# The last six modulation tiles are made in the norm chain before the second feed-forward half, from weights loaded in the mixer's output stage

## Chip, cores and metric

One core of a Trainium2 chip runs the whole layer. The metric is the time of one execution on the device in microseconds (us). Matrix products run on TensorE (PE in the rows), elementwise work on VectorE (DVE), ScalarE (ACT) and GpSimd (POOL); SyncE (SP) issues nearly all transfers, in the order of its queue.

## What is computed

One layer of a hybrid backbone: 512 latent tokens (x) and 256 context tokens, 1024 channels. A modulation vector of 9 × 1024 numbers is made from the conditioning c, and the layer is a half-step feed-forward block, a mixer, and a second half-step feed-forward block:

```python
mx = [m[:, None, :] for m in adaln(c, w_ada[i], b_ada[i])]   # silu(c) @ w_ada + b_ada, split in 9
x = x + 0.5 * mx[2] * swiglu(modulate(rmsnorm(x, norm1_w[i]), mx[0], mx[1]), ffn1_w_in[i], ffn1_w_out[i])
ux = modulate(rmsnorm(x, norm2_w[i]), mx[3], mx[4])
...
mix_x = merge_branches(px, pool_grid(px[..., GATE_END:POOL_END]), ox, ...)
x = x + mx[5] * mix_x
x = x + 0.5 * mx[8] * swiglu(modulate(rmsnorm(x, norm3_w[i]), mx[6], mx[7]), ffn2_w_in[i], ffn2_w_out[i])
...
return rmsnorm(x, final_norm_w)
```

The mixer's merge is `(g_pool * y_pool + g_gdn * y_gdn) @ w_mix_out`, where the g are sigmoids of a projection (the branch gates), y_pool is a projection by w_pool_proj and y_gdn one by w_gdn_proj. What matters here: the ninth modulation part, mx[8], is needed only when the second feed-forward block adds to x.

## The kernel before

**The modulation.** w_ada is cut into 72 tiles of 1024 × 128, 512 KB each; tile t gives 128 of the 9216 modulation numbers, so tiles 64 to 71 give mx[8]. `ada_steps` makes two tiles, a pair: it loads both (SP, line 146), multiplies them with the conditioning vector `sc` (line 150: 16 small matmuls, which the trace counts as 32, since each runs in two passes), copies the product (VectorE, line 153, buffer `ada`), and after its `yield` transposes it (line 157), reduces and adds the bias (lines 159 and 162). Eight pairs are made at the start. The other 28 pairs wait in the list `ada_left`. `trickle` is called in the first feed-forward half at fixed places and makes the next pair there, whose second part follows at the next call; `LATE` = 2 pairs are kept for the end of that half. `mod_gate(1, 2, True)` and `mod_gate(1, 8, True)` scale the gate parts of the two feed-forward halves into `eff`.

**The first feed-forward half** computes with matmuls at line 345 in groups of output channels; each precise product is three matmuls of a high and a low part (names ending in hi and lo). VectorE and ScalarE split weights and activations, GpSimd helps.

**The mixer's output stage.** The last 11 of the 16 branch gates are made in the last steps of the scan loop: matmuls of line 132 (operands hhi, hlo), ScalarE's copy to `bgate` (line 1032), SP's write to `bg_dram` (line 1033). Then the stage begins: four tiles of y are read back (yg, line 1078), split into yphi and yplo (lines 188 and 189) and multiplied with w_pool_proj, whose tiles are loaded at line 110 and split at lines 119 and 120; the gates come back as gp and gg (lines 1083 and 1095) and get their sigmoid. Further yg, from yg_dram (line 1089), feed w_gdn_proj, and at the end w_mix_out updates the stream xl, which was loaded whole (line 1091, 2 MB).

**The norm chain.** Squares of xl are gathered in acc (line 197); TensorE sums them over channels (line 205, on bank b), VectorE and GpSimd make the reciprocal root (lines 177 and 179), VectorE spreads it on a diagonal (`diag`, line 209), TensorE broadcasts it (line 215), and VectorE and ScalarE make nt, xhi and xlo from it, with which the second half begins (line 279). `f0` are its first weights, loaded ahead.

**What sets the order.** The code is traced once; a scheduler lays out each engine's queue from the order in the code and from when buffers come free, and each engine then runs its queue in that order. All loads and writes of these stages go through SP's one queue.

## Time and profile before

| | us |
|---|---|
| median of 3 runs | 1752.39 |
| lowest and highest run | 1749.08 to 1753.36 |
| the profiled execution's own time | 1756.71 |
| its span | 1755.0 |
| TensorE busy | 1653.5 (94%) |
| VectorE busy | 1119.0 (64%) |
| ScalarE busy | 842.6 (48%) |
| GpSimd busy | 390.8 (22%) |

The span is the stretch between the first and the last recorded instruction of the profiled execution; a little time lies around it. TensorE is busy nearly throughout, so the few places at which it stands are those to look at. PEclk in the rows is the granted clock of TensorE as a share of the full 2.4 GHz: 1.00 is the upper level, 0.50 the lower, 1.2 GHz; values between are stretches with both.

### The profile page before, as it was taken

To read this page: it belongs to the slowest core of one execution; us is meant where nothing else is said; L and a number is where in the kernel's file an instruction comes from. 1 tells how busy PE (TensorE), PEld (TensorE's weight loads), DVE (VectorE), ACT (ScalarE), POOL (GpSimd) and SP (SyncE) were. 2 spreads that over 40 slices of the span, in tenths; PEclk is the share of its full clock that TensorE was granted. 3 is DMA by queue.
4 is the path that set the end of the run, shared out by engine and by line. 5 is a ranking of instruction groups with operands and counts; after the bars stand their busy time and mean duration, and the time that the engine had idled before them with its cause. 6 is when DMAs were issued, how large, how long until landed. Compare 5 with 4: busy or idle time off the path is not lost.

```text
span 1755.0 us, 31315 instructions
## 1 busy us (share of the span) xinstructions
PE 1653.5 (94%) x12220; PEld 1423.9 (81%) x12220; DVE 1119.0 (64%) x2254; ACT 842.6 (48%) x1851; POOL 390.8 (22%) x493
## 2 busy tenths in 40 slices
PE   6899999999999999889999999999998999999996
PEld 4889898989999778777878788787786788888885
DVE  5778888798888886375678767774555533333333
ACT  5443343434444364667677767665443322222233
POOL 2243444444454121123323331100000000000000
PEclk9999999999999999989999999999999999999998
DMA  9355536361221325532112212224654232333321
GB/s 273 112 155 151 156 96 182 103 189 65 78 67 56 108 82 187 138 100 67 44 52 65 60 45 53 56 61 154 214 158 116 69 98 88 94 96 96 93 64 48
DMA packets 282696, 183.82 MB, mean 105 GB/s; under 512 B 7008, under 2 KB 269877, under 8 KB 282421
## 3 DMA queue, kind: packets, MB, share of 16 engines
q1 hardware_dynamic: 282112, 181.65, 35.6%
q8 instruction: 96, 1.57, 0.4%
q14 instruction: 51, 0.42, 0.1%
q10 hardware_dynamic: 437, 0.18, 0.1%
HBM read 170.22 MB, written 11.58 MB: 104 GB/s over the span
## 4 chain that ended last, share of the span: by engine, by line
PE 71%; DVE 14%; ACT 5%; DMA 5%; POOL 2%; issue 2%; SPq 0%; ACTq 0%; POOLq 0%; DVEq 0%
PE b L132 22%; PE b L345 9%; PE a L132 6%; PE g L132 6%; PE a L345 5%; PE g L345 5%; DVE cv L583 2%; PE b L279 2%; PE a L279 1%; PE g L279 1%; PE a L708 1%; ACT din L848 1%; DVE wlo L120 1%; DMA bg_dram<-bgate 1%; PE b L150 1%
## 5 line engine op out<-in xcount | busy, mean ns | idle before, releaser
L188 ACT CAST fhi<-fst 128x512 fp32r<-128x512 f32 (+1 forms) x136 | 77.7, 605 | 249.6 <-PE b L132 85.6
L132 PE MATMUL b<-hhi,whi 128*128 128x512 f32 (+1 forms) x528 | 187.6, 384 | 0.0
L132 PE MATMUL b<-hlo,whi 128*128 128x512 f32 (+1 forms) x528 | 187.5, 383 | 0.0
L132 PE MATMUL b<-hhi,wlo 128*128 128x512 f32 (+1 forms) x528 | 186.9, 384 | 0.0
L179 POOL TENSOR_TENSOR rs<-rs,mhalf 128x4 f32<-128x4 f32 (+2 forms) x13 | 13.6, 1045 | 665.3 <-DVE rs L177 649.7
L189 DVE TENSOR_TENSOR flo<-fst,fhi 128x512 fp32r<-128x512 f32 (+1 forms) x136 | 87.3, 671 | 92.6 <-ACT fhi L188 92.4
L119 ACT CAST whi<-stg 128x512 fp32r<-128x512 f32 x146 | 89.4, 620 | 91.6 <-PE b L132 59.9
L119 ACT CAST whi<-qst 128x512 fp32r<-128x512 f32 (+1 forms) x160 | 81.6, 512 | 106.5 <-PE b L345 43.2
L119 ACT CAST whi<-qs 128x512 fp32r<-128x512 f32 (+1 forms) x120 | 59.5, 512 | 115.2 <-POOL qs L309 76.2
L583 DVE SCALAR_TENSOR_TENSOR cv<-raw,vec,cv 128x772 f32<-128x772 f32 (+1 forms) x96 | 101.6, 1058 | 11.6 <-ACT cv L581 8.3
L120 DVE TENSOR_TENSOR wlo<-qst,whi 128x512 fp32r<-128x512 f32 (+1 forms) x160 | 100.7, 639 | 10.1 <-ACT whi L119 10.0
L132 PEld LDWEIGHTS b<-hlo,whi 128*128 128x128 f32 x528 | 94.0, 190 | 14.8
L132 PEld LDWEIGHTS b<-hhi,whi 128*128 128x128 f32 x528 | 94.0, 190 | 14.8
L132 PEld LDWEIGHTS b<-hhi,wlo 128*128 128x128 f32 x528 | 93.3, 190 | 14.8
L308 POOL TENSOR_TENSOR qs<-qst 128x512 f32<-128x512 f32 (+1 forms) x40 | 46.4, 1161 | 247.2 <-DMA qst<-in_ffn_w_in_dram 76.6
L120 POOL TENSOR_TENSOR wlo<-stg,whi 128x512 fp32r<-128x512 f32 x46 | 65.4, 1430 | 90.6 <-ACT whi L119 70.6
L120 DVE TENSOR_TENSOR wlo<-stg,whi 128x512 fp32r<-128x512 f32 x100 | 68.2, 686 | 22.1 <-ACT whi L119 20.2
L188 ACT CAST ahi<-q 128x384 fp32r<-128x384 f32 x74 | 37.5, 512 | 75.4 <-DVE q L257 35.6
L120 DVE TENSOR_TENSOR wlo<-qs,whi 128x512 fp32r<-128x512 f32 (+1 forms) x80 | 49.0, 613 | 32.6 <-ACT whi L119 32.6
L132 PE MATMUL b<-xlo,fhi 128*128 128x512 f32 x160 | 63.4, 396 | 0.0
L132 PE MATMUL b<-xhi,flo 128*128 128x512 f32 x160 | 63.4, 396 | 0.0
L132 PE MATMUL b<-xhi,fhi 128*128 128x512 f32 x160 | 63.4, 396 | 0.0
(512 smaller groups left out, 4909.8 us busy)
## 6 DMA issues: line engine op xcount, KB each, us to landing
stg<-in_w_ada_dram SPq DMA_DIRECT2D x56, 512.0 KB, 4.0
stg<-in_w_mix_in_dram SPq DMA_DIRECT2D x49, 512.0 KB, 3.7
fst<-in_ffn_w_in_dram SPq DMA_DIRECT2D x44, 512.0 KB, 3.6
qst<-in_ffn_w_in_dram SPq DMA_DIRECT2D x40, 512.0 KB, 3.4
qst<-in_ffn_w_out_dram SPq DMA_DIRECT2D x40, 256.0 KB, 2.6
adx<-in_w_ada_dram SPq DMA_DIRECT2D x16, 512.0 KB, 6.4
fst<-in_ffn_w_out_dram SPq DMA_DIRECT2D x16, 512.0 KB, 3.9
crow<-cumd SPq DMA_DIRECT2D x16, 384.0 KB, 7.8
```

What stands on the lines that cost most here:

```text
L119: (first.copy if first is act else first.tensor_copy)(out=hi[:, :n], in_=w)
L120: second.tensor_tensor(out=lo[:, :n], in0=w, in1=hi[:, :n], op=ALU.subtract)
L132: pe.matmul(res[p][:, :m], lhsT=ww(i), rhs=hh(k)[:, o:o + m], start=(i == 0 and j == 0), stop=(i == n - 1 and j == 2))
L150: pe.matmul(b[32 * j:32 * j + 32, e * 128:(e + 1) * 128], lhsT=sc[:, k, :], rhs=stg[:, k, :], start=(i == 0), stop=(i == 1))
L188: act.copy(out=hi, in_=src)
L189: dve.tensor_tensor(out=lo, in0=src, in1=hi, op=ALU.subtract)
L279: pe.matmul(x, lhsT=ww(k), rhs=rhs(j, part, k), start=n + e == 0, stop=n + e == len(ks) + 1)
L308: pool.tensor_tensor(out=s1, in0=a21, in1=a22, op=ALU.add)
L345: pe.matmul(o, lhsT=ww[:, k], rhs=rhs(j, part, k), start=first and k + i == 0, stop=k + i == nh + 1, skip_group_check=not first)
L583: dve.scalar_tensor_tensor(out=cv[:, :n], in0=raw[:, t:t + n], scalar=tap[t], in1=cv[:, :n], op0=ALU.mult, op1=ALU.add)
L708: pe.matmul(r[:, :256], lhsT=hh[:, k, t * 128:(t + 1) * 128], rhs=ww[:, k], start=n == 0, stop=n == 3 * KT - 1)
L848: act.copy(out=din[o:o + 32, :, 0:12].rearrange("p f u -> p u f"), in_=L[o:o + 32, :, o:o + 32])
```

## The change

Tiles 66 to 71 leave `ada_left`, which now has 25 pairs, so three trickled pairs fewer are made in the first half (the number 24 in `trickle` becomes 21, so that the first gate is scaled after the same pair). Their six loads of 512 KB each are issued in the mixer's output stage into buffers of their own (pool `al`). In the norm chain the matmuls of the three pairs are put in fixed places: the first pair ahead of the sums, the second between the sums and the broadcast, the third behind the broadcast. Their transposes, reductions and additions follow after the first two hidden tiles of the second half are activated, and `mod_gate(1, 8, True)` after them. The copies of the products and `diag` are put into the loaded tiles, where these are done with; `sc` moves to a pool that lives to the end.

```diff
--- before.py
+++ after.py
@@ -82,7 +82,7 @@
     pool.memset(ones, 1.0)
     mhalf = base.tile([128, 32], F32, name="mhalf")
     pool.memset(mhalf, -0.5)
-    sc = xs.tile([128, KT, 32], F32, name="sc")
+    sc = base.tile([128, KT, 32], F32, name="sc")
     pool.memset(sc, 0.0)
     vb = bank("a")
     pe.transpose(vb[:, 0:16], cvec, ident[0:16, 0:16])
@@ -138,24 +138,29 @@
         for _ in ada_steps(cts, tags, room):
             pass
 
-    def ada_steps(cts, tags="bb", room=None):
+    def ada_steps(cts, tags="bb", room=None, loaded=None):
         b = bank(tags[0])
         for e, t in enumerate(cts):
-            pl_, tag, bufs = room or (wp, "stg", 2)
-            stg = pl_.tile([128, KT, 128], F32, tag=tag, name=tag, bufs=bufs)
-            sp.dma_start(out=stg, in_=a["w_ada"][:, t * 128:(t + 1) * 128].rearrange("(k p) m -> p k m", p=128))
+            if loaded:
+                stg = loaded[e]
+            else:
+                pl_, tag, bufs = room or (wp, "stg", 2)
+                stg = pl_.tile([128, KT, 128], F32, tag=tag, name=tag, bufs=bufs)
+                sp.dma_start(out=stg, in_=a["w_ada"][:, t * 128:(t + 1) * 128].rearrange("(k p) m -> p k m", p=128))
             for i in range(2):
                 for j in range(4):
                     k = 2 * j + i
-                    pe.matmul(b[32 * j:32 * j + 32, e * 128:(e + 1) * 128], lhsT=sc[:, k, :], rhs=stg[:, k, :],
-                              start=(i == 0), stop=(i == 1))
-        s = xs.tile([128, 256], F32, tag="ada", name="ada", bufs=1)
+                    ins = pe.matmul(b[32 * j:32 * j + 32, e * 128:(e + 1) * 128], lhsT=sc[:, k, :], rhs=stg[:, k, :],
+                                    start=(i == 0), stop=(i == 1))
+                    if loaded and i + j == 0:
+                        tc.keep_in_program_order(ins)
+        s = loaded[0][:, 0:2].rearrange("p k m -> p (k m)") if loaded else xs.tile([128, 256], F32, tag="ada", name="ada", bufs=1)
         dve.tensor_copy(out=s, in_=b[:, :256])
         yield
         b2 = bank(tags[1])
         for i in range(2):
             pe.transpose(b2[:, i * 128:(i + 1) * 128], s[:, i * 128:(i + 1) * 128], ident)
-        r = xs.tile([128, 2, 2], F32, tag="adar", name="adar", bufs=2)
+        r = (room if loaded else xs).tile([128, 2, 2], F32, tag="adar", name="adar", bufs=2)
         dve.tensor_reduce(out=r, in_=b2[:, :256].rearrange("p (t j s) -> p t s j", t=2, j=4)[:, :, :2, :],
                           axis=AX.X, op=ALU.add)
         for i, t in enumerate(cts):
@@ -196,15 +201,20 @@
             act.activation(out=sq, in_=src, func=AF.Square)
             dve.tensor_tensor(out=acc[:, :n], in0=acc[:, :n], in1=sq, op=ALU.add)
 
-    def rstd_rows(tmp, acc, parts, ssq=None, tag="b", dtag=("diag", 1)):
+    def rstd_rows(tmp, acc, parts, ssq=None, tag="b", dtag=("diag", 1), meanwhile=None, diag=None):
 
         n = sum(PARTS[p][1] for p in parts)
         if ssq is None:
             ssq = bank(tag)
             for i in range(n // 128):
-                pe.matmul(ssq[:, i:i + 1], lhsT=acc[:, i * 128:(i + 1) * 128], rhs=ones[:, 0:1])
+                ins = pe.matmul(ssq[:, i:i + 1], lhsT=acc[:, i * 128:(i + 1) * 128], rhs=ones[:, 0:1])
+                if meanwhile and not i:
+                    tc.keep_in_program_order(ins)
+        if meanwhile:
+            meanwhile()
         r = rstd_of(ssq[:, :n // 128], n // 128, D)
-        diag = tmp.tile([128, n], F32, tag=dtag[0], name="diag", bufs=dtag[1])
+        if diag is None:
+            diag = tmp.tile([128, n], F32, tag=dtag[0], name="diag", bufs=dtag[1])
         for i in range(n // 128):
             dve.tensor_scalar(out=diag[:, i * 128:(i + 1) * 128], in0=ident, scalar1=r[:, i:i + 1],
                               scalar2=None, op0=ALU.mult)
@@ -212,7 +222,9 @@
         for p in parts:
             m = PARTS[p][1]
             bs[p] = bank(tag)
-            pe.matmul(bs[p][:, :m], lhsT=ones, rhs=diag[:, o:o + m])
+            ins = pe.matmul(bs[p][:, :m], lhsT=ones, rhs=diag[:, o:o + m])
+            if meanwhile:
+                tc.keep_in_program_order(ins)
             o += m
         return bs
 
@@ -527,14 +539,14 @@
     w_first = []
     x_dram = dr.tile([128, KT, LAT], F32, name="x_dram")
     LATE = 2
-    ada_left = [(t, t + 1) for t in range(16, 72, 2)]
+    ada_left = [(t, t + 1) for t in range(16, 66, 2)]
 
     ada_open = []
 
     def trickle():
         for g in ada_open:
             next(g, None)
-            if len(ada_left) == 24:
+            if len(ada_left) == 21:
                 mod_gate(1, 2, True)
         ada_open.clear()
         if len(ada_left) > LATE:
@@ -1060,6 +1072,12 @@
     xs2 = ctx.enter_context(tc.tile_pool(name="xs2", bufs=1, reuse_waits="tile"))
     xl = xs2.tile([128, KT, LAT], F32, name="xl")
     acc2 = xs2.tile([128, LAT], F32, name="acc2")
+    al = ctx.enter_context(tc.tile_pool(name="al", bufs=1, reuse_waits="tile"))
+    ada_last = []
+    for t in range(66, 72):
+        stg = al.tile([128, KT, 128], F32, name=f"al{t}")
+        sp.dma_start(out=stg, in_=a["w_ada"][:, t * 128:(t + 1) * 128].rearrange("(k p) m -> p k m", p=128))
+        ada_last.append(stg)
     mg_cm = tc.tile_pool(name="mg", bufs=1, reuse_waits="tile")
     mg = mg_cm.__enter__()
 
@@ -1132,8 +1150,10 @@
     f0 = [tile_weights(w_in, 0, KT, c) for c in (0, FF, 128, FF + 128)]
     for k in range(KT):
         mod_scale(2, k, 7, R_N3)
-    mod_gate(1, 8, True)
-    rb = rstd_rows(mn, acc2, ONLY)["lat"]
+    last = [ada_steps((t, t + 1), tags, al, ada_last[t - 66:t - 64]) for t, tags in ((66, "ba"), (68, "bg"), (70, "ga"))]
+    next(last[0])
+    rb = rstd_rows(mn, acc2, ONLY, meanwhile=lambda: next(last[1]), diag=ada_last[0][:, 4:8].rearrange("p k m -> p (k m)"))["lat"]
+    next(last[2])
     banks = [bank(tag) for tag in "aagg"]
     steps = side_by_side(f0, [[b] for b in banks], lambda _, part, k: (xhi, xlo)[part][:, k], range(KT))
     for k in range(KT):
@@ -1168,6 +1188,9 @@
 
     for f in range(2):
         activated(f, banks[2 * f], banks[2 * f + 1])
+    for g in last:
+        next(g, None)
+    mod_gate(1, 8, True)
     for i, (g0, g1) in enumerate(GROUPS):
         for f in range(max(g0, 2), g1):
             project_in(f)
```

**SP, from the branch gates into the output stage.** Before; bg_dram<-bgate are the writes of the gates, of which the last is the third here, yg what the first matmuls of the stage are made from:

```order
L1078 DMA yg<-y_dram 128x512 x2
L1083 DMA gp<-bg_dram 128x512 x2
L1091 DMA xl<-x_dram 128x4096
L1017 DMA yg_dram<-y 128x512
L1033 DMA bg_dram<-bgate 128x512
L110 DMA stg<-in_w_pool_proj_dram 128x4x128 x2
L1095 DMA gg<-bg_dram 128x512
L1033 DMA bg_dram<-bgate 128x512
L1095 DMA gg<-bg_dram 128x512
L110 DMA stg<-in_w_pool_proj_dram 128x4x128 x2
L1033 DMA bg_dram<-bgate 128x512
```

After; al_14444 to al_14454 are the six tiles 66 to 71:

```order
L1045 DMA bg_dram<-bgate 128x512
L110 DMA stg<-in_w_pool_proj_dram 128x4x128 x2
L1045 DMA bg_dram<-bgate 128x512
L110 DMA stg<-in_w_pool_proj_dram 128x4x128
L1079 DMA al_14444<-in_w_ada_dram 128x8x128
L1079 DMA al_14446<-in_w_ada_dram 128x8x128
L1079 DMA al_14448<-in_w_ada_dram 128x8x128
L1079 DMA al_14450<-in_w_ada_dram 128x8x128
L1079 DMA al_14452<-in_w_ada_dram 128x8x128
L1079 DMA al_14454<-in_w_ada_dram 128x8x128
L1096 DMA yg<-y_dram 128x512 x2
L1101 DMA gp<-bg_dram 128x512 x2
```

The first yg and gp loads moved from ahead of the last three gate writes to behind the last one, and the six new loads stand between.

**TensorE, from the last mixer matmuls into the second half.** Before; acc is summed, diag broadcast:

```order
L132 MATMUL b<-hlo,whi 128x512
L132 MATMUL b<-hhi,wlo 128x512
L205 MATMUL b<-ones,acc_14530 128x1 x4
L215 MATMUL b<-diag,ones 128x512
L279 MATMUL a<-xhi,fhi 128x512 x2
L279 MATMUL g<-xhi,fhi 128x512 x2
L279 MATMUL a<-xlo,fhi 128x512
L279 MATMUL a<-xhi,flo 128x512
```

After (line 153 is the old 150, 210 and 225 the old 205 and 215, 291 the old 279; the broadcast's operand is the same diag, kept in tile 66):

```order
L132 MATMUL b<-hlo,whi 128x512
L132 MATMUL b<-hhi,wlo 128x512
L153 MATMUL b<-al_14444,sc 32x128 x8
L153 MATMUL b<-al_14446,sc 32x128 x8
L210 MATMUL b<-ones,acc_14440 128x1 x4
L153 MATMUL b<-al_14448,sc 32x128 x8
L153 MATMUL b<-al_14450,sc 32x128 x8
L225 MATMUL b<-al_14444,ones 128x512
L153 MATMUL g<-al_14452,sc 32x128 x8
L153 MATMUL g<-al_14454,sc 32x128 x8
L291 MATMUL a<-xhi,fhi 128x512 x2
L291 MATMUL g<-xhi,fhi 128x512 x2
```

Two tiles now stand ahead of the sums, two between sums and broadcast, two behind it.

## Rows read from the trace of the kernel before

**Rows 1.** The page, part 4: the chain that ended last, share by engine.

```profile
PE 71%; DVE 14%; ACT 5%; DMA 5%; POOL 2%; issue 2%; SPq 0%; ACTq 0%; POOLq 0%; DVEq 0%
```

**Rows 2.** Timeline, TensorE: start us, us, operation, out<-in, count, [idle before].

```profile
365.11 0.38 PE L157 MATMUL b<-ident,ada 128*128 128x128 f32 x2
365.42 1.08 PE L150 MATMUL b<-stg,sc 128*32 128x128 f32 x32
366.43 0.44 PE L345 MATMUL g<-ahi,whi 128*128 128x384 f32 x1
...
386.95 0.44 PE L157 MATMUL b<-ident,ada 128*128 128x128 f32 x2 [1.51 <-DVE ada L153]
```

**Rows 3.** Windows of line 150: us, PE and PEld busy, clock, DMA.

```profile
244.06:348.84 104.78, 9.29 (x256) 6.66 (x256) 0.98 0.48 141
348.84:448.77 99.93, 5.61 (x160) 4.00 (x160) 1.00 0.38 117
448.77:543.02 94.25, 0.00 (x0) 0.00 (x0) 1.00 0.21 68
```

**Rows 4.** Timeline, SP's queue, mixer output stage.

```profile
1216.53 0.99 SPq L1078 DMA_DIRECT2D yg<-y_dram  x2
...
1233.63 0.93 SPq L110 DMA_DIRECT2D stg<-in_w_pool_proj_dram  x2
1236.12 0.34 SPq L1033 DMA_DIRECT2D bg_dram<-bgate  x1
...
1239.03 0.94 SPq L1078 DMA_DIRECT2D yg<-y_dram  x2
```

**Rows 5.** Timeline, TensorE, end of the branch gates.

```profile
1234.58 0.40 PE L132 MATMUL b<-hhi,wlo 128*128 128x512 f32 x1
1238.26 0.79 PE L132 MATMUL b<-yphi,whi 128*128 128x512 f32 x1 [3.28 <-ACT yphi L188]
```

**Rows 6.** Timeline, ScalarE, third yg.

```profile
1242.14 0.62 ACT L188 CAST yphi<-yg 128x512 fp32r<-128x512 f32 x1 [3.42 <-DMA yg<-y_dram]
```

**Rows 7.** Timeline, VectorE, weight split in the output stage.

```profile
1231.48 0.69 DVE L120 TENSOR_TENSOR wlo<-stg,whi 128x512 fp32r<-128x512 f32 x1 [3.79 <-ACT whi L119]
```

**Rows 8.** Windows: us, five engines busy, PEclk, DMA share, GB/s.

```profile
20.00:25.00 5.00, 3.61 (x45) 2.10 (x43) 4.66 (x13) 3.82 (x8) 0.69 (x1) 1.00 1.21 290
1220.00:1225.00 5.00, 5.00 (x25) 3.94 (x24) 1.10 (x3) 4.68 (x12) 1.22 (x2) 1.00 1.01 380
1238.00:1244.00 6.00, 5.73 (x12) 3.76 (x13) 2.61 (x5) 1.95 (x4) 0.00 (x0) 0.50 0.40 131
1250.00:1265.00 15.00, 15.00 (x67) 12.40 (x67) 9.53 (x16) 9.18 (x16) 0.00 (x0) 1.00 0.94 291
```

**Rows 9.** Chain of waits, 1258 to 1272: start us, us, what.

```profile
1261.44 5.92 DMA yg<-yg_dram
```

**Rows 10.** Timeline, TensorE, norm chain and start of the second half.

```profile
1354.86 1.05 PE L205 MATMUL b<-ones,acc 128*128 128x1 f32 x8 [2.29 <-DVE acc L197]
1358.23 2.07 PE L215 MATMUL b<-diag,ones 128*128 128x512 f32 x2 [2.31 <-DVE diag L209]
1361.90 1.22 PE L279 MATMUL a<-xhi,fhi 128*128 128x512 f32 x2 [1.59 <-ACT xhi L1143]
...
1367.03 0.39 PE L279 MATMUL a<-xhi,fhi 128*128 128x512 f32 x1
1367.26 0.40 PE L279 MATMUL a<-xlo,fhi 128*128 128x512 f32 x1
```

**Rows 11.** Windows, columns as in rows 8.

```profile
1357.00:1358.00 1.00, 0.00 (x0) 0.00 (x0) 0.70 (x4) 0.00 (x0) 0.26 (x1) 0.50 0.00 0
51.00:55.00 4.00, 1.98 (x11) 1.58 (x11) 4.00 (x7) 2.95 (x6) 2.50 (x3) 1.00 0.67 167
...
578.00:581.00 3.00, 3.00 (x12) 3.00 (x12) 3.00 (x4) 1.12 (x3) 1.93 (x2) 0.56 0.03 5
```

**Rows 12.** Timeline, TensorE, one modulation tile in the start stage.

```profile
29.35 1.08 PE L150 MATMUL a<-adx,sc 128*32 128x128 f32 x16
```

## The prediction

> **What bounds the kernel now.** First the shares of the chain that ended last: matmuls hold 71% of the span, VectorE 14%, transfers 5% [rows 1]. So a change here is worth what it does to TensorE's stream, and one look decides at each place: does TensorE arrive and find its operand, or does it stand? The change touches four places. In the first feed-forward half TensorE runs without holes around a modulation pair [rows 2], so what is taken out there comes off the end. In the output stage of the mixer it stands once, for 3.28 us, between the last matmul of the branch gates at 1234.58 and the first w_pool_proj matmul at 1238.26 [rows 5], and then runs full: 15.00 of 15 us busy between 1250 and 1265 [rows 8]. In the norm chain before the second feed-forward half it mostly stands, because one small step waits for the next [rows 10]. At the start of that half it runs densely again. So work that goes into the norm chain may be free, and anything that lengthens the one pause in the output stage is paid in full, since the dense work behind it has no slack in which to catch up.
>
> **Part 1, taken out of the first feed-forward half: three pairs.** A dense pair shows its cost directly: two transposes start at 365.11, the 32 small matmuls at 365.42, and the down-projection goes on at 366.43 [rows 2]. That is 0.31 + 1.01 = 1.32 us, and the first matmul behind has a pitch some 0.1 longer: 1.42. A second reading compares three like stretches, each from the first matmul of one output group to that of the next: with 256 of the small matmuls (eight pairs) one lasts 104.78 us, with 160 (five pairs) 99.93, with none 94.25 [rows 3]; (104.78 − 94.25)/8 = 1.32 and (99.93 − 94.25)/5 = 1.14. Three pairs are 4.3 by the dense rows, 3.9 and 3.4 by the stretches; I take **−4.0**. Up to −5.5 is possible if the 1.51 us in which the transposes at 386.95 wait for VectorE's copy of the modulation product [rows 2] goes as well; I leave that out, because VectorE is the busy one at that place and its queue would make the next matmul wait instead. The low end is −3.4.
>
> **Part 2, the loads in the output stage.** The same six loads of 512 KB are issued later, so the amount is unchanged; what counts is who stands behind them on SP's queue. Before, SP has issued the first two yg loads at 1216.53, long before the last gate's write at 1236.12 [rows 4], and what TensorE needed first after the gates was in SBUF. In the order of the changed kernel the six loads stand right behind the last gate's write and its w_pool_proj load, and the first yg loads come behind all six. TensorE's next matmul needs the cast of the first yg. So the pause becomes a chain: gate copy, write, six loads, yg, cast.
>
> When does it begin? The order puts three weight casts ahead of the last gate's copy on ScalarE. The third cast's tile is loaded when the split at 1231.48 (0.69) [rows 7] has ended, so at about 1232.2 instead of 1233.63 [rows 4]. With 3.3 us to land (the 3.1 found below and 0.2 for the load beside it), 0.6 for the cast, 0.6 for the copy and 0.5 for two issues, the first of the six is issued at about 1237.2 (an estimate from these rows). From issue to data: the yg issued at 1239.03 [rows 4], with nothing ahead of it, is cast at 1242.14 [rows 6], 3.1 us, of which 0.9 is moving 256 KB at 290 GB/s; so 2.2 us pass before data move. The six are 3.146 MB. The nearest rows for their rate are those of w_ada loads alone: 290 GB/s from 20 to 25 us [rows 8], so 10.85 us. Then 0.9 for the first yg and 0.6 to the matmul: 1237.2 + 2.2 + 10.85 + 0.9 + 0.6 = 1251.7 against 1238.26, **+13.4**. Behind the restart nothing new comes: the third and fourth yg wait for a free buffer as before, and the sigmoids that ScalarE now does there lie beside the nine matmuls that need only the first two yg; at worst one of them costs 0.6. The clock was at its lower level behind the pause already, 0.50 from 1238 to 1244 [rows 8].
>
> Bounds: the rate of 380 GB/s, which the load of xl shows [rows 8], makes the six 8.3 us and the term +10.8; xl's rows are far longer than w_ada's, so I stay with the w_ada row. One more 512 KB at 290 GB/s ahead of yg makes +15.2. Below: zero, if yg is not held at all; that is the rival below. That a small load does wait behind others on this queue, one row shows: 256 KB of yg issued at 1261.44 took 5.92 us [rows 9], twice the 3.1 above, with other loads ahead of it.
>
> The Trainium skill, page "DMA: Bandwidth & Descriptors", section "Queues, rings and completion order", says two things here: that each engine takes the descriptors of one ring in their order, and that completion is not first in, first out per issuing engine. By the second alone yg could land beside the six, and the time would be that of the first rival; the 5.92 us above is on the side of the first. The same page's section "Bandwidth" has 341 GB/s for transfers of 1 MB; by that the six would take 9.2 us and the whole would come out at about 1758.1, but the trace's own rate for these very loads is lower.
>
> **Part 3, the norm chain.** Before, TensorE ends its last mixer matmul at 1352.6 and then has only the sums at 1354.86 and the broadcast at 1358.23 until 1361.90 [rows 10]. The clock is granted at 0.50 from 1357 [rows 11], the lower level; the broadcast takes 2.07 us and the first twelve matmuls of the second half 1361.90 to 1367.03, 5.13 us, where 0.235 each, about the pitch from 1367.03 on, would be 2.82 [rows 10]. The change puts a pair of tiles ahead of the sums, one between sums and broadcast, one behind the broadcast, each about 1.0 us at the upper level [rows 2] and 2.1 at the lower, by one tile's 16 matmuls at 29.35, which took 1.08 where 32 take that at the upper level [rows 2, 12]. The first fits before the sums (TensorE idle 2.29 us [rows 10]), the second beside VectorE, GpSimd and diag (sums end 1355.9, broadcast from 1358.23). The extra copy of the first pair stands before the last addition of squares on VectorE, where VectorE waits for ScalarE's squares anyway; the sums wait for that addition [rows 10], so I keep 0 to 0.2.
>
> If the clock stays at the upper level, the broadcast takes 1.03 instead of 2.07, the twelve matmuls 2.82 instead of 5.13, and the third pair fits beside nt and xhi: −1.04 − 2.31 + 0.15 for copies = **−3.2**. If it falls as before, the third pair runs 2.1 us from 1360.3 and ends behind 1361.90: +0.5. Which? From 51 to 55 us TensorE was busy 1.98 of 4 us and the clock stayed at 1.00; from 578 to 581 it was busy throughout and shows 0.56, after a stretch with holes [rows 11]. In the new chain it works about 2.6 of the 5 us from 1353 to 1358, a share like that of the row that stayed. I take the upper level, not with much confidence.
>
> **Part 4, start of the second half.** Six transposes, 3 × 0.31 [rows 2], plus some 0.07 of pitch each, now stand inside dense matmuls: **+1.1** (1.0 to 1.4). Reductions, additions and the gate go to VectorE, which nobody waits for there until the first down-projection; nil. Moving sc to another pool and diag into the tile of the first pair adds no wait of a later date; nil.
>
> **Sum.** −4.0 + 13.4 − 3.2 + 1.1 = +7.3. The profiled execution took 1756.71 us with a span of 1755.0, 4.3 above the median of the runs; against its own time that is 1764.0, and against the median 1752.39 it is 1759.7.
>
> **Rivals.**
> - *The loads hold nobody.* If yg goes past the six or shares the engines so that it lands within the old pause, part 2 is 0: −4.0 − 3.2 + 1.1 = −6.1, **1746.3**, faster than before. For it: transfers are only 5% of the chain and yg is small. Against: one queue, the order, and rows 9. It decides the sign: with the other terms, any hold under 6.1 us is a gain.
> - *The clock falls in the norm chain as before.* −4.0 + 13.4 + 0.5 + 1.1 = +11.0, **1763.4**. For it: two empty stretches of over 1 us remain. Against: the row at 51 us.
> - *The six move at xl's rate.* +10.8 in part 2, +4.7 in all, **1757.1**, no change that can be told.
> - *The first half keeps its length*, since VectorE paces it and the three pairs filled its holes: +11.3, **1763.7**. For it: the wait at 386.95; against: the stretches without pairs are shorter [rows 3].
>
> **How the numbers follow.** Forecast 0.42, no hold 0.12, clock falls 0.25, fast loads 0.13, first half unchanged 0.08. About 0.3% (5.3 us) is what a measurement of this kernel can tell from no change, so slower begins at 1757.7. Of the forecast some 0.7 lies above that, of the fallen clock and of the unchanged first half nearly all, of the fast loads 0.4: 0.65 together. Faster comes from the no-hold case alone, 0.11. The rest, 0.24, is within. The range goes from 1750 to 1766.5: the low end takes in fast loads with the larger gain of part 1, the high end the fallen clock with 15.2 for part 2; what is left out is mostly the no-hold case.
>
> **What would show it.** TensorE's pause after the last gate should be near 16.7 us, ended by the cast of yg, with SP's six w_ada issues ahead of yg's; a pause under 5 us refutes part 2. The no-modulation look of the first half should extend three pairs further and its end come 4 to 5 us earlier. From 1357 on (in old time) the granted clock should read 1.00 and the broadcast near 1.03 us; 0.50 there means the fallen clock.

## The result and the profile after

The changed kernel takes 1766.41 us (median; 1759.89 to 1771.94), the kernel before 1752.2 beside it. The ratio is 1.0086, with a 95% interval of 1.0065 to 1.0108: about 15 us slower. The forecast was 1759.7, 7.3 us slower. The sign holds, the size is twice what was forecast, and the range, whose upper end is 1766.5, holds by 0.1 us. The profiled execution took 1766.23 us, its span is 1764.5.

The work has not grown. Section 1 of the page of the changed kernel gives each engine's busy time, and TensorE's 1653.3 us is that of before (1653.5). The two profiled executions differ by 9.5 us in their spans (that of the kernel before was itself 4.3 us above its median), and all of that is time in which TensorE stands:

```profile
PE 1653.3 (94%) x12220; PEld 1425.2 (81%) x12220; DVE 1115.4 (63%) x2254; ACT 843.2 (48%) x1851; POOL 390.6 (22%) x493
```

**Where it stands: the output stage.** Timeline of SP's queue in the changed kernel (start us, us, line, out<-in, count); it answers [rows 4]:

```profile
1234.03 0.34 SPq L1045 DMA_DIRECT2D bg_dram<-bgate  x1
1234.47 0.37 SPq L110 DMA_DIRECT2D stg<-in_w_pool_proj_dram  x1
1234.89 7.93 SPq L1079 DMA_DIRECT2D al<-in_w_ada_dram  x6
1242.87 2.18 SPq L1096 DMA_DIRECT2D yg<-y_dram  x2
```

Timeline of TensorE, the answer to [rows 5]:

```profile
1232.70 0.40 PE L132 MATMUL b<-hhi,wlo 128*128 128x512 f32 x1
1249.78 0.79 PE L132 MATMUL b<-yphi,whi 128*128 128x512 f32 x1 [16.68 <-ACT yphi L193]
```

The chain of waits of the changed kernel in between (start us, us, what) ends like this, behind six pieces of SPq L1079 of 0.55 to 1.75 us:

```profile
1242.87 6.22 DMA yg<-y_dram
...
1249.11 0.63 ACT yphi L193
```

And the windows of the changed kernel (columns as in [rows 8]) show a stretch in which only the queue works:

```profile
1238.00:1246.00 8.00, 0.00 (x0) 0.00 (x0) 0.00 (x0) 0.00 (x0) 0.00 (x0) 0.50 1.15 292
```

This is the second part of the forecast as it was told: the last gate's write, six loads at 292 GB/s, yg behind all of them, the cast, and TensorE back after 16.68 us, where it stood 3.28 before: 13.40 us more. From 1215 us to the restart the trace is 14.75 longer; the other 1.35 lie ahead of the pause, where the transposes of the last head now stand earlier in TensorE's order and wait for ot.

**The norm chain.** Timeline of TensorE in the changed kernel, against [rows 10]; L153 are the three pairs, L210 the sums, L225 the broadcast, L291 the second half:

```profile
1365.14 1.05 PE L210 MATMUL b<-ones,acc 128*128 128x1 f32 x8 [1.28 <-DVE acc L202]
1366.12 1.93 PE L153 MATMUL b<-al,sc 128*32 128x128 f32 x32
1368.50 2.07 PE L225 MATMUL b<-al,ones 128*128 128x512 f32 x2 [0.45 <-DVE al L219]
1370.51 1.94 PE L153 MATMUL g<-al,sc 128*32 128x128 f32 x32
1372.37 0.99 PE L291 MATMUL a<-xhi,fhi 128*128 128x512 f32 x2
```

Its windows, against [rows 11]:

```profile
1366.00:1373.00 7.00, 6.55 (x70) 3.88 (x70) 3.26 (x10) 1.38 (x2) 1.01 (x1) 0.51 0.00 0
1373.00:1376.00 3.00, 3.00 (x14) 2.28 (x13) 2.87 (x5) 1.05 (x2) 0.00 (x0) 1.00 0.02 5
```

The clock fell all the same: two of the pairs take 1.93 us instead of 1.08 and the broadcast 2.07 as before. It was at the lower level from 1366.1 to 1372.95, 6.8 us, where the kernel before had 10.2 us from 1356.6 on. So it came back before the second half, whose first matmuls run at the upper level; from the last mixer matmul to there the chain is 1.7 us shorter, not 3.2.

**The first half and what follows it.** Windows of the kernel before: the first feed-forward half from one of its matmuls to the end of its down-projection, and the stretch of the mixer from a w_mix_in matmul to the transposes of qf in line 771, which end a wait of 8.99 us:

```profile
330.20:606.86 276.66, 265.24 (x1632) 255.19 (x1632) 237.35 (x446) 117.37 (x249) 115.97 (x107) 0.99 0.29 89
710.21:749.28 39.07, 30.08 (x147) 23.91 (x145) 10.67 (x18) 25.01 (x61) 8.67 (x20) 0.95 0.57 143
```

The same two, between the same instructions, in the changed kernel:

```profile
326.42:599.76 273.34, 261.89 (x1529) 253.96 (x1529) 232.90 (x434) 117.36 (x248) 114.35 (x107) 0.99 0.25 78
703.44:743.72 40.28, 30.13 (x146) 23.92 (x145) 10.66 (x18) 24.82 (x61) 8.68 (x20) 0.93 0.62 134
```

The first is 3.32 us shorter, 1.1 for each pair, with the DMA rate down as six loads are gone. The second does the same work in 1.21 us more. The forecast knew nothing of that, and many of the experiments below look into it.

### The profile page after: what moved, and what is told of

It is laid out like the page before. It is cut to its first block, busy times and chain, and to the rows that moved or that the text cites. A ratio compares the mean times of both kernels' runs of the same rounds, so it can differ in the third digit from the quotient of the medians.

```text
span 1764.5 us, 31310 instructions
## 1 busy us (share of the span) xinstructions
PE 1653.3 (94%) x12220; PEld 1425.2 (81%) x12220; DVE 1115.4 (63%) x2254; ACT 843.2 (48%) x1851; POOL 390.6 (22%) x493
## 4 chain that ended last, share of the span: by engine, by line
PE 72%; DVE 15%; ACT 5%; DMA 4%; issue 2%; POOL 2%; SPq 1%; POOLq 0%; ACTq 0%; DVEq 0%
PE b L132 24%; PE b L357 8%; PE g L132 6%; PE a L132 6%; PE g L357 5%; PE a L357 5%; DVE cv L595 2%; PE b L291 2%; PE a L720 1%; PE g L291 1%; DVE wlo L120 1%; DVE xT L449 1%; ACT din L860 1%; PE b L153 1%; PE g L985 1%
## 5 line engine op out<-in xcount | busy, mean ns | idle before, releaser
L449 DVE SCALAR_TENSOR_TENSOR xT<-q,eff,xT 128x128 f32<-128x128 f32 (+2 forms) x100 | 63.7, 658 | 0.1
```

Of the source, the lines that this page charges most:

```text
L449: dve.scalar_tensor_tensor(out=r[:, o0:o1], in0=c[i][j][:, o0 - j * n2:o1 - j * n2], scalar=gate(m + i, s), in1=r[:, o0:o1], op0=ALU.mult, ...
```

## Experiments

Each kernel was timed beside the kernel before on one chip. The kernels ran on several chips, so only the ratios can be compared with each other; medians of two rows can have different neighbours. The timed runs list the mean granted clock too, which matters below: among the runs of one kernel, taken over all kernels, 0.001 of it goes with about 1.1 us.

| kernel | median us | ratio to before, 95% | mean clock, timed runs |
|---|---|---|---|
| before, beside the runs below | 1752.4 to 1753.9 | | 0.9822 |
| b_again | 1754.47 | 1.0006 [0.9995, 1.0016] | 0.9814 |
| a_again | 1769.05 | 1.0083 [1.0068, 1.0098] | 0.9786 |
| p1 | 1755.59 | 1.0015 [1.0004, 1.0026] | 0.9810 |
| p2 | 1768.06 | 1.0083 [1.0069, 1.0097] | 0.9776 |
| p34 | 1752.79 | 1.0002 [0.9991, 1.0013] | 0.9827 |
| late | 1754.09 | 1.0002 [0.9988, 1.0016] | 0.9820 |
| p2tiny | 1757.88 | 1.0033 [1.0021, 1.0046] | 0.9811 |
| p1fill | 1753.00 | 0.9998 [0.9986, 1.0011] | 0.9816 |
| p1d6 | 1756.32 | 1.0020 [1.0003, 1.0037] | 0.9802 |
| bd2 | 1753.23 | 0.9997 [0.9983, 1.0012] | 0.9822 |
| p1dve | 1754.81 | 1.0015 [1.0000, 1.0029] | 0.9814 |
| p1pad | 1755.69 | 1.0017 [1.0005, 1.0029] | 0.9805 |
| p1load | 1757.17 | 1.0028 [1.0014, 1.0041] | 0.9795 |
| late_d6 | 1754.97 | 1.0021 [1.0005, 1.0036] | 0.9807 |
| late_pad | 1757.26 | 1.0021 [1.0002, 1.0040] | 0.9812 |
| late_load | 1757.68 | 1.0025 [1.0014, 1.0036] | 0.9807 |
| bfill | 1750.72 | 0.9983 [0.9968, 0.9997] | 0.9857 |
| latefill | 1752.11 | 1.0003 [0.9989, 1.0017] | 0.9841 |

### Both kernels again

> The kernel before, unchanged. Its first profiled execution took 1756.71 us, 4.3 above the median of its runs. Theory A: that execution was simply a slow one, in which TensorE's clock fell at places where it usually doesn't; this one is then nearer to 1752, with fewer stretches at the lower clock, and the places of the falls differ from the first. Theory B: the falls sit at fixed places; then the trace shows the same ones. The ratio to itself is 1.000 within 0.002.

> The changed kernel, unchanged. Theory A: 1764 to 1768 us, the pause after the branch gates again 16.7 us, the norm chain again partly at the lower clock, and between 600 and 900 us no fixed loss against before. Theory B: the 3.3 us that the first trace lost there against before come again at the same places.

Neither has an edit. The kernel before repeats within 0.1%, which bounds what a single comparison here can tell. Its mean clock reads 0.9814 in that repeat, 0.0007 under that of the runs beside it, with nothing changed. The changed kernel stands at 1.0083 again, with a pause of 17.28 us.

### The parts one by one

p1 leaves the three pairs out, and the last gate is scaled from part 7 of the modulation in place of part 8:

```
-    ada_left = [(t, t + 1) for t in range(16, 72, 2)]
+    ada_left = [(t, t + 1) for t in range(16, 66, 2)]
...
-    mod_gate(1, 8, True)
+    mod_gate(1, 7, True)
```

> The kernel before with tiles 66 to 71 left out (the last gate takes part 7 of the modulation instead of part 8): part 1 of the prediction alone. Prediction: -4.0 us, 1748.2 (between -3.4 and -5.5). Rival (VectorE paces that half): 0, 1752.

p2 puts the six loads into the kernel before, read by nobody:

```
+    al = ctx.enter_context(tc.tile_pool(name="al", bufs=1, reuse_waits="tile"))
+    ada_last = []
+    for t in range(66, 72):
+        stg = al.tile([128, KT, 128], F32, name=f"al{t}")
+        sp.dma_start(out=stg, in_=a["w_ada"][:, t * 128:(t + 1) * 128].rearrange("(k p) m -> p k m", p=128))
+        ada_last.append(stg)
     mg_cm = tc.tile_pool(name="mg", bufs=1, reuse_waits="tile")
```

> The kernel before with only the pool of six tiles and their six loads added at the place where the changed kernel has them; nobody reads them. Prediction, part 2 alone: +13.4, 1767; with the 1.3 us that the first trace of the changed kernel shows for the transposes of the last head, 1768.5. Rival (the pause comes from reading the tiles later): no change, 1754.

TensorE's timeline in p2 shows the pause, with the loads read by nobody:

```profile
1252.81 0.80 PE L132 MATMUL b<-yphi,whi 128*128 128x512 f32 x1 [17.40 <-ACT yphi L188]
```

p34 keeps all 28 pairs in the first half and makes the last three once more in the norm chain, from loads behind the output stage. Against the kernel before, in parts:

```
-    mod_gate(1, 8, True)
...
+    last = [ada_steps((t, t + 1), tags, al, ada_last[t - 66:t - 64]) for t, tags in ((66, "ba"), (68, "bg"), (70, "ga"))]
+    next(last[0])
-    rb = rstd_rows(mn, acc2, ONLY)["lat"]
+    rb = rstd_rows(mn, acc2, ONLY, meanwhile=lambda: next(last[1]), diag=ada_last[0][:, 4:8].rearrange("p k m -> p (k m)"))["lat"]
+    next(last[2])
...
+    for g in last:
+        next(g, None)
+    mod_gate(1, 8, True)
```

> All 28 pairs stay in the first half, and the norm chain makes tiles 66 to 71 once more, from loads in the w_mix_out stage: parts 3 and 4 alone. Prediction: -3.2 + 1.1 = -2.1, 1751.8. From the first trace of the changed kernel (clock falls in the chain, but recovers sooner): -1.7 + 0.9 = -0.8, 1753.1. Fallen clock as in the rival: +1.6, 1755.5.

By their ratios part 1 costs 2.6 us (0.7 to 4.6), part 2 14.5 (12.1 to 17.0), parts 3 and 4 together 0.3 (-1.6 to 2.3). That is 17.4 against 14.6 to 15.1 for the whole, which is inside what these intervals leave. Part 1 can be had in a second way: late, which is described next, has parts 1, 3 and 4, p34 has parts 3 and 4, and both stand at 1.0002, so the difference is 0.0 us (about -3 to 3). Against the forecast (-4.0, +13.4, -2.1), part 2 was nearly right, and what was to be gained elsewhere did not come.

### Part 2: bytes or order

late moves the pool al and its loads of the changed kernel behind the output stage, to where the pool fw is opened, and leaves all else:

```
-    al = ctx.enter_context(tc.tile_pool(name="al", bufs=1, reuse_waits="tile"))
-    ada_last = []
...
     mg_cm = tc.tile_pool(name="mg", bufs=1, reuse_waits="tile")
...
     fw = ctx.enter_context(tc.tile_pool(name="fw", bufs=1, reuse_waits="tile"))
+    al = ctx.enter_context(tc.tile_pool(name="al", bufs=1, reuse_waits="tile"))
+    ada_last = []
...
```

> As the changed kernel, but the pool of the six tiles is opened only when the first feed of the second half is set up, so that it takes no memory from the output stage and SP issues the six loads in the w_mix_out stage. Theory A (the pause is the six loads ahead of yg, and pool and queue alone make it): the pause is back at 3.3 us, the transposes of the last head wait no more, 13.4 + 1.3 us go, 1751 to 1752. Forecast of the prediction without its part 2: 1746.3. Rival (the loads cost as much wherever they are issued): above 1760, with a new pause in the w_mix_out stage.

TensorE's timeline in late has the pause back at its old size, and 14 us of the 15 are gone:

```profile
1234.72 0.49 PE L132 MATMUL b<-yphi,whi 128*128 128x512 f32 x1 [2.27 <-ACT yphi L193]
```

p2tiny keeps p2's pool, its six DMAs and every engine's order, and cuts the bytes:

```
-        sp.dma_start(out=stg, in_=a["w_ada"][:, t * 128:(t + 1) * 128].rearrange("(k p) m -> p k m", p=128))
+        sp.dma_start(out=stg[0:1, 0, :], in_=a["w_ada"][0:1, t * 128:(t + 1) * 128])
```

> Part 2 alone (the six tiles and their pool at the start of the mixer's output stage), with each load of 512 KB cut to one row of 512 bytes: the buffers, the number of DMAs and the order of every engine are those of part 2 alone, the 3 MB are gone. Transfer theory (yg waits behind 3 MB on one queue, the forecast's step): TensorE's pause at the first product of yphi falls from 17.4 to 4 to 6 us, and the time is 0 to 3 us over the kernel before, 1.000 to 1.002. Memory theory (the pool al takes memory that comes free early, and yg has to wait for memory that comes free late): the pause stays over 10 us and the time 8 us or more over the kernel before, 1.005.

SP's queue in p2tiny, to be held against 7.93 us for the six in the changed kernel:

```profile
1231.98 1.90 SPq L1067 DMA_DIRECT2D al<-in_w_ada_dram  x6
1233.92 1.08 SPq L1084 DMA_DIRECT2D yg<-y_dram  x2
```

And its pause on TensorE:

```profile
1237.17 0.79 PE L132 MATMUL b<-yphi,whi 128*128 128x512 f32 x1 [6.99 <-ACT yphi L188]
```

The pause of 17.40 in p2 becomes 6.99, so 10.4 us are the bytes. The other 3.7 over the 3.28 of before stay without them, and the time stays 5.8 us (3.7 to 8.1) over the kernel before: yg is still issued behind the last gate's write, where SP issued its first two loads at 1216.53 before [rows 4]. This is the part of the 13.4 that the forecast counted without saying what made it. In late, with al opened later, yg is early again. Why it moves is not shown. The author's account is that the pool al takes memory that comes free early and leaves yg's buffers with memory that comes free late; but al's own six loads are issued only at 1231.98, behind the last gate's write at 1231.11, and yg may be late only because it stands behind them on SP's queue. No run separates the two. Neither of the two expectations named the mixture, and the measured 1.0033 lies between them.

### Where the gain of part 1 goes

The first stretch of the windows above is 3.1 to 3.5 us shorter in p1, late, and both executions of the changed kernel than in that trace of the kernel before, yet none of these is faster than the kernel before. All the traces together show a smaller gain: 275.8 to 279.3 us (mean 277.1) in the seven kernels that keep the pairs, 273.2 to 278.0 (mean 274.8) in the twelve that have neither the pairs nor p1fill's work in their place. In four of these twelve (p1d6, p1pad, late_pad, late_load) the stretch is 276.0 to 278.0, hardly shorter than in the kernel before, with 6.8 to 10.2 us of it at the lower clock. So part of the gain is lost to the clock where it arises. p1's windows show more of it given back in the second stretch:

```profile
328.60:601.78 273.18, 260.85 (x1530) 252.52 (x1529) 231.73 (x434) 117.08 (x248) 114.66 (x107) 0.99 0.25 78
704.87:745.66 40.79, 30.14 (x147) 23.92 (x145) 10.66 (x18) 24.81 (x61) 8.67 (x20) 0.92 0.53 127
```

3.48 us are won and 1.72 lost again with the same work in it. (The second stretch is 37.7 to 39.1 in the seven kernels with the pairs; the trace of the kernel before is the longest of them.) Two waits make this loss. One is ScalarE's step df in line 730. In the kernel before it goes on when the product g is there:

```profile
713.83 0.69 ACT L730 ACTIVATE df<-g,vec 128x512 f32<-128x512 f32 x1 [1.76 <-PE g L132]
```

In p1 it starts about 1.0 us later than its product, which is ready at 708.38, allows:

```profile
709.42 0.69 ACT L730 ACTIVATE df<-g,vec 128x512 f32<-128x512 f32 x1 [2.70 <-PE b L132]
```

The wait is put down to the last event that the profile could name, but bank b is no operand of df. The same step in p1load (further below) names the other thing that df needs:

```profile
713.96 0.69 ACT L737 ACTIVATE df<-g,vec 128x512 f32<-128x512 f32 x1 [2.02 <-DMA y_dram<-df]
```

df is written into the buffer whose last contents SP is still writing to y_dram (256 KB, which land in 16 parts). In p1 that write is issued at 704.28, 15 parts have landed at 707.00 and the sixteenth at 709.32; df starts 0.10 us later. In all 20 traces 15 parts land 2.7 to 3.9 us after the issue. The sixteenth lands with them in the seven kernels with the pairs and in p1fill (2.9 to 3.8 us) and later in the other twelve (3.9 to 5.1), and the same two groups of traces differ in when the next 16 KB of code for TensorE (queue "q8 instruction" of the profile) is fetched (up to there 36 fetches where TensorE has 4615 or, in p1pad and late_pad, 4621 records, and 35 where it has 4513): 3.4 to 4.1 us after the write's issue in the eight, 1.3 to 2.7 us after it, while the write is under way, in the twelve. So the late part goes with a fetch of code that falls into the write. That is a coincidence in 20 traces; no run moves the fetch alone.

The other is crow, the rows of cumd copied to all partitions, which ScalarE needs for the decays. ScalarE's timeline in the kernel before, the first two uses:

```profile
735.81 1.86 ACT L817 ACTIVATE arg<-crow,ncumc 128x128 f32<-128x128 f32 x6 [4.03 <-DMA crow<-cumd]
740.68 0.40 ACT L817 ACTIVATE arg<-crow,ncumc 128x128 f32<-128x128 f32 x1 [3.01 <-DMA crow<-cumd]
```

In p1:

```profile
732.37 1.86 ACT L817 ACTIVATE arg<-crow,ncumc 128x128 f32<-128x128 f32 x6 [5.08 <-DMA crow<-cumd]
738.53 0.40 ACT L817 ACTIVATE arg<-crow,ncumc 128x128 f32<-128x128 f32 x1 [4.29 <-DMA crow<-cumd]
```

Counted from the issue of first16, the DMA of SP's queue just ahead of crow's, the second use comes after 13.8 to 15.0 us in the seven kernels with the pairs and after 15.2 to 16.5 in p1, late, the changed kernel and its repeat. No single late part like that of df's write is found there. Since arrival does not decide it (p1d6 comes there 2.4 us later than p1 and loses no less), the next runs put back one by one what the pairs brought.

p1fill puts back TensorE's work, on data at hand, without loads and without VectorE's share:

```
...
+    fills = [0, 1, 2]
+
+    def fill_steps():
+        b = bank("b")
+        for e in range(2):
+            for i in range(2):
+                for j in range(4):
+                    pe.matmul(b[32 * j:32 * j + 32, e * 128:(e + 1) * 128], lhsT=sc[:, 2 * j + i, :], rhs=ident,
+                              start=(i == 0), stop=(i == 1))
+        yield
+        b2 = bank("b")
+        for i in range(2):
+            pe.transpose(b2[:, i * 128:(i + 1) * 128], ident, ident)
...
+        elif fills:
+            ada_open.append(fill_steps())
+            next(ada_open[0])
+            fills.pop()
```

> Tiles 66 to 71 left out as in the run of part 1 alone, but where the three pairs stood TensorE does the same number of small matmuls and transposes on the identity: no loads, nothing on VectorE. Theory C (without the pairs TensorE has holes there in front of VectorE, its clock falls oftener, and that eats the 4 us): about the time of before, 1752 to 1754, and not 4 us above the run of part 1 alone (1755.6). Theory D (VectorE paces that stretch, TensorE's work there is free): the time of the run of part 1 alone, 1755.6. Theory E (the loss of that run has nothing to do with TensorE there): 4 us above it, 1759 to 1760.

By time it stands at 0.9998, without p1's loss. The intervals of the two overlap, but all five kernels of part 1 without this work (p1 and the four that follow, 1.0015 to 1.0028) lie above the upper end of p1fill's, 1.0011. df is on time again; crow is not (second use after 16.2 us).

p1d6 puts back the count of DMAs with loads of 512 bytes:

```
+    tiny = lambda: [sp.dma_start(out=wp.tile([128, KT, 128], F32, tag="stg", name="stg", bufs=2)[0:1, 0, :], in_=a["w_ada"][0:1, 0:128]) for _ in range(2)]
...
+        elif tinies: tinies.pop(), tiny()
```

bd2 adds two loads of 128 bytes to the kernel before, issued at 47.8 us; two more shift the count modulo eight as six fewer do:

```
+    tiny = lambda: [sp.dma_start(out=dum[:, i], in_=a["w_ada"][0:1, 0:32]) for i in range(2)]
...
-    mod_gate(3, 5, False)
+    tiny(); mod_gate(3, 5, False)
```

> Part 1 alone again (tiles 66 to 71 are never made), but where each of the three pairs had its two loads of 512 KB, two loads of 512 bytes into the same buffers are issued and never read, so that the DMAs of the whole kernel keep their count and every later one its place in the count. TensorE, VectorE and ScalarE have the order of part 1 alone. Count theory (what part 1 gains in the first half, 3.5 us, is given back at 716 and 735 to 760 us because six DMAs fewer stand in front, which moves every later DMA by six places): the wait of the transposes of line 771 for kt is 8 to 9 us as in the kernel before (9.9 in part 1 alone), nothing is given back there, and the time is 3 to 3.5 us under the kernel before (0.998). Traffic theory (it is the bytes or the work of the pairs that matter, or the earlier arrival itself): the wait stays at 9.9, and the time is that of part 1 alone, 1755.6 (1.0015).

> The kernel before with two loads of 128 bytes more on SP's queue, near its start, read by nobody; the order of all other engines is untouched. Part 1 takes six DMAs out, and two more is the same shift in a rotation of eight. Count theory: nothing changes before 690 us, the wait of line 771 for kt grows from 8.6 to about 10, the stretch 735 to 760 is 1.2 to 2.1 us longer, and the time 1.5 to 2.5 us over the kernel before (1.001). Traffic theory: no difference anywhere, ratio 1.000 within 0.001.

Both speak against the count: p1d6 is as slow as p1 with crow at 16.6 us, and bd2 changes nothing, with crow at 13.9.

The next two ask whether it matters where the engines' code lies: leaving the pairs out takes instructions of VectorE and TensorE out too, and moves all that follow. p1dve adds twelve small copies on VectorE near the start to p1, p1pad those and 54 one-column matmuls in the pairs' places. This is p1pad's edit in parts; p1dve's `pad` has the copies alone:

```
+    def pad():
+        for n in (16, 2):
+            pb = bank("b")
+            for i in range(n):
+                pe.matmul(pb[0:32, 0:1], lhsT=sc[:, 0, :], rhs=ident[:, 0:1], start=True, stop=True)
+        for i in range(4):
+            dve.tensor_copy(out=spare[:, i, :], in_=mods[:, 0, :])
...
+        elif pads: pads.pop(), pad()
```

> Part 1 alone, with 12 copies of 16 bytes a partition on VectorE more, near the kernel's start and read by nobody: VectorE's code from there to the end stands at the places that it has in the kernel before (leaving the three pairs out takes 12 VectorE and 54 TensorE instructions out). Code theory (part 1's gain is given back at 735 to 760 us because VectorE's code moved: the 8 KB code load that stands at 696 us in the kernel before stands at 714 in every kernel without the pairs, the one with TensorE filler among them): the second copy of the gap's row table lands as in the kernel before (ScalarE's second use of crow 13.8 to 15.0 us after the load of first16, 15.2 to 16.6 without the pairs), the wait of line 771 is under 9.3 us, and the time is 1.5 to 2 us under part 1 alone, 1754 (1.000). Rival, that the work or the loads themselves matter: crow as in part 1 alone, 1755.6 (1.0015).

> As p1dve, and 54 TensorE instructions of one column more where the three pairs stood, in two buffers of tag b for each pair as there: TensorE's code and its use of PSUM stand as in the kernel before too, at about a quarter of the pairs' time. Code theory: besides crow, the extra 0.6 us of ScalarE at 716 us goes, nothing is given back between 690 and 760 us, and what the first half gains (2 to 3 us) is kept: 1750.5 to 1752 (0.9985 to 0.9993). Rival: 1755 to 1756 (1.001 to 1.0015).

The wait of df is all but gone in both (0.05 and 0.13 us are left of it): the stretch from 710 to 735 us is as before (+0.01 in p1dve). crow lands earlier than in p1 but not as before (15.2 and 15.5). By time both are as slow as p1. In both the sixteenth part of the write is still late, 4.2 us after its issue, so putting VectorE's code back did not bring it back in time, and by time the code's place decides nothing.

p1load is p1dve with six full loads, read by nobody, in the pairs' places:

```
...
+        for _ in range(2):
+            stg = wp.tile([128, KT, 128], F32, tag="stg", name="stg", bufs=2)
+            sp.dma_start(out=stg, in_=a["w_ada"][:, 0:128].rearrange("(k p) m -> p k m", p=128))
...
```

> p1dve (part 1 alone, VectorE's code at its old places) with the three pairs' six loads of 512 KB left in and read by nobody: of the three pairs only TensorE's matmuls and VectorE's evacuations are missing. Load theory (the slower landing of crow at 735 to 740 us comes with the bytes or descriptors of six full loads left out): ScalarE's second use of crow is back at 13.8 to 15.0 us after the load of first16, nothing is given back between 690 and 760 us, and the first half's gain of 3 us shows by time: 1749 to 1750.5 (0.998 to 0.999). Work theory (it is TensorE's matmuls of the pairs themselves whose absence costs, by the clock or by earlier arrival): crow at 15.2 or later, and the time that of p1dve, 1754 to 1755 (1.001 to 1.0015).

ScalarE's timeline in p1load: the second use of crow comes 14.4 us after first16, as with the pairs.

```profile
736.85 1.87 ACT L824 ACTIVATE arg<-crow,ncumc 128x128 f32<-128x128 f32 x6 [5.03 <-DMA crow<-cumd]
741.36 0.40 ACT L824 ACTIVATE arg<-crow,ncumc 128x128 f32<-128x128 f32 x1 [2.65 <-DMA crow<-cumd]
```

Its windows:

```profile
329.76:605.19 275.43, 262.42 (x1529) 253.68 (x1529) 232.53 (x433) 116.87 (x247) 115.19 (x107) 0.99 0.30 89
710.09:748.48 38.39, 30.16 (x147) 23.95 (x145) 10.66 (x18) 24.79 (x61) 8.67 (x20) 0.96 0.48 139
```

The second stretch is 0.68 us shorter than before: crow's give-back is gone, as the load theory says, and of df's 0.25 us are left. But the time is the worst of the family, 1.0028, and the load theory's 1749 to 1750.5 falls with it. Its first stretch was only 1.23 shorter in this execution, and the timed runs have the lowest clock of the family, 0.9795.

The same three cures on late, parts 1, 3 and 4 of the change together:

> The changed kernel with its six loads at the start of the mixer's output stage put behind that stage (as in late) and with six loads of 512 bytes in the first half where those of the three pairs stood. Count theory: the gain of the first half is kept, 3 us under late, about 1751 us, 0.998 of the kernel before. Traffic theory: as late, 1754.1 and 1.000.

> The changed kernel with its six loads behind the output stage (late) and with p1pad's idle instructions where the three pairs stood. Code theory: 2 to 3 us under late, 1751 to 1752 (0.999). Rival: as late, 1754.1 (1.000).

> The changed kernel with its six loads behind the output stage (late), VectorE's code at its old places, and six loads of 512 KB read by nobody where the three pairs stood. Load theory: the first half's gain is kept, 2.5 to 3 us under late, 1750 to 1751 (0.9985). Work theory: as late, 1753 to 1754 (1.000).

None of them makes late faster: 1.0021, 1.0021 and 1.0025 against 1.0002, if anything the other way. late_load agrees on crow (15.0 us, against 16.5 in late). It disagrees on df: with VectorE's copies in it, 0.9 us are lost there again: the write's sixteenth part lands 5.08 us after its issue, with a fetch of TensorE's code 2.65 us after it.

What the family says together: the five kernels of part 1 that lack TensorE's work of the pairs (p1, p1d6, p1dve, p1load, and p1pad with its 54 matmuls of one column) have a mean clock of 0.9795 to 0.9814 in their timed runs, each under the 0.9822 of the kernel before, on average by 0.0017. At 1.1 us for 0.001 that is 1.9 us of what is lost. The unchanged b_again with its 0.9814 warns that a single one of these means says little. The one kernel of part 1 that keeps TensorE at work in full in those places, p1fill, has the time of before and the clock of the runs beside it (0.9816 against 0.9818). The place of the falls changes from one execution to the next: between the same instructions, 749 to 1000 us, the two profiled executions of the kernel before differ by 3.0 us with nothing changed. The Trainium skill, page "TensorE: Matmul & The Clock Gate", section "Part 1: The HAM clock gate", says that the count of slow matmuls varies from run to run of one kernel. These two traces agree: 6.6 us of that stretch are at the lower level in one and 15.8 in the other. So a single trace cannot show which falls the missing matmuls cause, and that link is argued from the means and from p1fill, not shown.

### The clock in the norm chain

bfill is the kernel before with 28, 28 and 16 idle matmuls on the identity (two records each) in the three gaps of the norm chain, and nothing moved:

```
...
+    def warm(n):
+        for i in range(n):
+            ins = pe.matmul(wb[32 * (i % 4):32 * (i % 4) + 32, 0:128], lhsT=ident[:, 0:32], rhs=ident, start=True, stop=True)
+            if not i:
+                tc.keep_in_program_order(ins)
...
+    rb = rstd_rows(mn, acc2, ONLY, warm=warm)["lat"]
```

`rstd_rows` calls warm(28) ahead of the sums, warm(28) behind them and warm(16) behind the broadcast.

> The kernel before with idle matmuls on the identity in the three gaps of the norm chain (28 ahead of the sums, 28 between sums and broadcast, 16 behind it), about 2 us, 2 us and 1 us of TensorE work with no loads and no VectorE work. If work in the gaps holds the clock at the upper level: the broadcast takes 1.03 us and the first twelve matmuls 2.8, -3.3 us, 1750.6. If it falls all the same: 0 to +1, 1754 to 1755.

TensorE's timeline in bfill, against [rows 10]:

```profile
1350.11 1.74 PE L1149 MATMUL g<-ident 128*32 128x128 f32 x56
1352.47 1.05 PE L207 MATMUL b<-ones,acc 128*128 128x1 f32 x8 [0.62 <-DVE acc L197]
1353.46 1.74 PE L1149 MATMUL g<-ident 128*32 128x128 f32 x56
1355.84 1.13 PE L221 MATMUL b<-diag,ones 128*128 128x512 f32 x2 [0.65 <-DVE diag L215]
1356.90 1.08 PE L1149 MATMUL g<-ident 128*32 128x128 f32 x32
1358.56 0.74 PE L288 MATMUL a<-xhi,fhi 128*128 128x512 f32 x2 [0.58 <-ACT xhi L1160]
```

The broadcast takes 1.13 and the chain is 3.16 us shorter: the forecast's -3.2 for part 3 is right for a chain whose clock stays up. The gain is there by time as well, 0.9983 (0.9968 to 0.9997), 2.4 us under the kernel it was timed beside, with the highest clock of all. This kernel beats both.

latefill gives late's three pairs 20 idle matmuls each:

```
+        if loaded:
+            for i in range(20):
+                ins = pe.matmul(b[32 * (i % 4):32 * (i % 4) + 32, 256:384], lhsT=ident[:, 0:32], rhs=ident, start=True, stop=True)
...
```

> The changed kernel with its six loads behind the output stage (late), and 20 idle matmuls on the identity ahead of each of the three pairs in the norm chain, 0.6 us each time. If the forecast's step on the clock only failed because the pairs are too short for the gaps: no fall of the granted clock between 1350 and 1380 us, the chain 1 to 1.5 us shorter than in late, and as in bfill (0.9983) a time 2 to 3 us under late, 1751 to 1752 (0.999). If the fall comes whatever fills the gaps: as late, 1754.1 (1.000).

TensorE's timeline in latefill, against the changed kernel's 0.45 to 1.28 us of idle time and 1.93 for a pair:

```profile
1350.88 1.05 PE L215 MATMUL b<-ones,acc 128*128 128x1 f32 x8 [0.19 <-DVE acc L207]
1351.86 1.30 PE L145 MATMUL b<-ident 128*32 128x128 f32 x40
1352.97 1.06 PE L158 MATMUL b<-al,sc 128*32 128x128 f32 x32
1354.24 1.13 PE L230 MATMUL b<-al,ones 128*128 128x512 f32 x2 [0.21 <-DVE al L224]
```

No fall there: with more work in the same gaps the clock stays up in this trace. The chain is 2.6 us shorter than before (2.0 in late). By time no gain shows: latefill stands at 1.0003 and late at 1.0002, each against the kernel before on its own chip, where 0.999 was expected. The 0.6 us by which the two chains differ are too little to tell, and its higher mean clock, 0.9841, did not become time.

## Why the prediction was right in sign and wrong in size

**Part 1, -4.0: the term that failed.** The step that failed is "what is taken out there comes off the end". By time part 1 alone is 2.6 us slower (0.7 to 4.6), and by late against p34 it is 0.0, so the term is off by 4.0 to 6.6. In its own stretch the working nearly held: 3.32 us are gone in the changed kernel and 3.15 in its repeat, 1.1 a pair, just short of the low end of 3.4. (Of the two readings of [rows 3], the 1.32 comes from a stretch whose granted clock is 0.98, where the others have 1.00; the 1.14 without that is what came.) Behind it, the traces of p1, late, the changed kernel and its repeat show 0.5 to 0.8 us come back at df, where a write's last part lands late, and 0.7 to 1.6 at crow, which putting the six loads back undoes. Measured as a mean, not traced to a place: a lower clock, 1 to 3 us, some of it in the first half itself. The rival "the first half keeps its length" gives 1763.7, close to the result, but its mechanism is not the one seen: in the changed kernel the half became shorter. Four of the other kernels without the pairs do keep its length, by the clock and not by VectorE. What stays open is how leaving out TensorE's matmuls lowers the clock, why six loads less make crow late, and why p1load, with hardly anything of either wait, is no faster for it.

**Part 2, +13.4: right.** The pause is 16.68 us where 16.7 was forecast, ended by the cast of yg, with six issues ahead of yg's, all as told. That it fits to 0.02 is in part luck: the first of the six was issued 2.19 us behind the last gate matmul, not 2.62, and from there to the restart it took 14.89, not 14.5. The yg at 1239.03, from which the 3.1 us were read, had not "nothing ahead of it" either: SP had issued a w_pool_proj load at 1238.43. The stretch is 14.75 longer, because the transposes of the last head wait 1.35 longer; they stand in the order, and the sum left them out. Of the like pause in p2, 10.4 us are bytes and 3.7 order. The rivals "the loads hold nobody" and "the six move at xl's rate" fall. The rule of the Trainium skill's page "DMA: Bandwidth & Descriptors", section "Queues, rings and completion order", that a ring's descriptors are taken in order agrees with the 6.22 us of yg behind the six.

**Part 3, -3.2: the clock was wrong.** The chain became 1.7 us shorter in the changed kernel, 1.2 in its repeat. "I take the upper level" rested on one row in which TensorE was half busy and the clock stayed; in this chain it fell too, 3.3 us after the last mixer matmul (4.0 before), and stayed down for 6.8 us instead of 10.2. The rival had the fall, but at +0.5 was too dark: the clock is back before the second half, which is most of the -1.7. bfill and latefill show in their traces that -3.2 and -2.6 are there if the gaps are filled; by time bfill shows it, latefill does not.

**Part 4, +1.1: a little less**, 0.7 in the changed kernel, its repeat and late.

**The sum** by the measured parts is 2.6 + 14.5 + 0.3 = 17.4, the whole 14.6 to 15.1. Against the forecast that is 6.6 us by part 1, 1.1 by part 2 and 2.4 by parts 3 and 4, 10.1 in all, where the whole misses by 7.3 to 7.8; the rest lies inside the intervals, and with part 1 at 0.0 (late against p34) nothing is left over. That 1766.41 still falls inside the range is luck: the upper end was made for a clock that falls as before and one more load ahead of yg, and what came was a part 1 that gives nothing back.
